# A hybrid encoder block on one core: four PSUM banks each for gates and projections, two lasting value tiles, and values projected last

## The chip, the cores and the metric

The kernel runs on one core of a Trainium2 chip. The metric is the device time of one execution in microseconds (us), from the first to the last instruction and the little around them. The kernel before takes 2870.84 us as the median of 3 runs (2866.83 to 2875.58 us).

The engines of the core are written as in the profile: PE multiplies matrices and adds up in PSUM, PEld loads its weights, DVE, ACT and POOL compute on tiles, SP issues most of the DMA transfers and POOL issues some. PSUM is used here as eight banks of 128 x 512 f32.

## The reference

One layer of an encoder block: 2048 tokens, 1024 channels. The part that the change touches is the input projection and what reads it:

```
xn   = rmsnorm(h, norm_mix_g)
proj = xn @ w_in                                   # 1024 -> 2560 columns
q, k, v, u, y = split(proj, [512, 1024, 1536, 2048])
q, k = rope(q), rope(k)                            # 8 heads x 64
attn = dilated_mixture_attention(q, k, v)          # windows 128/1, 512/4, 2048/16
uc   = centred_depthwise_conv(u, conv_w, conv_b)   # width 4
rec  = bidirectional_rglru(uc, gates ...) * gelu(y)
h    = h + concat([attn, rec]) @ w_out
h    = h + memory_cross_attention(...)             # 256 memory tokens
h    = h + squared_relu_mlp(...)                   # 4096 hidden
```

The two gates of `bidirectional_rglru` are block-diagonal products of `uc` with small weights, for two directions; after them come exponentials and two scans over the sequence.

## The kernel before, in words

**Arithmetic.** Every product of two f32 matrices is made of three matmuls on a high and a low part of each operand (`mm3`, lines 118 to 121: high by high, high by low, low by high). So one output bank of 128 x 512 over 1024 channels takes 8 x 3 = 24 matmuls.

**Stage one, the input projection (about the first 700 us).** The 2048 tokens are held as transposed activations `xh`, `xl` in two blocks of 1024 tokens, block 0 and block 1. Each block has two halves of 512 tokens. The 2560 columns are cut into ten units of 256 columns: two U units and two Y units for the recurrence, and two units each of values (v0, v1), keys (k0, k1) and queries (q0, q1). Each of the last six serves four heads. A unit loads its weights, splits them into `wh` (ACT, L225) and `wl` (POOL or DVE, L226), and then projects:

- `out_unit` (L390) writes one bank of 128 columns x 512 tokens in 24 matmuls. A U or Y unit takes four of them, each read by one DVE instruction (L409) and stored.
- `qk_unit` takes two outputs, `pa` and `pb`, for each half, and calls `rope` (L371 to L388). DVE reads the two banks four times (L376 to L379), adds up (L380, L381); then, for each of two results, ACT makes the high part `rh` (L385), DVE the low part `rl` (L386), and SP stores both (L387, L388) to `q_d` or `k_d` in DRAM. `rh` and `rl` have two buffers each.
- `v_unit` (L431 to L461) goes in four steps of 256 tokens. A step fills one bank in two parts (48 matmuls on 256 columns), DVE scales it into `v` (L451), POOL sets two columns of ones in a tile `vb` (L454), ACT writes the high halves into `vb` (L456), DVE the low ones (L457), and SP stores `vb` to `v_d` (L460). `vb` has one buffer: the memset of a step waits until the stores of the step before it have read the tile.

**The order of the units.** `block` (L575) runs a list of units over one block of tokens. The main sequence (L607 to L637) is: block 0 with U and Y; block 1 with U; the memory's keys and values; block 1 with Y, then the list `QKV` (L573); block 0, loaded a second time, with `QKV` without its last unit; the rest of the recurrence; the loads of head 0; block 0 with the last unit of `QKV`; and then the attention. So the last unit in the list is also the last work on PE before the attention.

**The recurrence beside it.** `lru` (L463 to L547) is a generator: each step of a Y, V, K or Q unit draws 1.3 of its steps. One of its steps is `gates` (L497): two groups of three matmuls, each into a bank of the tag "a", read by ACT (L513 into `tr`, L516 into `ti`), then exponentials on ACT and two DVE products (L520, L521). Other steps are the convolution (L489, L491), the scans (L531, L536) and the final product with the Y branch (L544), stored to `rec_d`.

**PSUM banks.** `psum_phase` opens a set of banks by tag; a tag's tiles rotate over its banks, and a new tile waits until the old tile's readers are done. In stage one the tags are `m0`, `m1`, `b`, `a`, two banks each. A projection asks for "mmb" and gets `m0`, `m1`, `b` in turn, so projections rotate over six banks; the gates have the two of "a". The memory's keys and values use "mm" (`m0`, `m1`) and "b". The profile writes `m` for both `m0` and `m1`.

**What sets the order.** No table of instructions is written out. A tile scheduler orders each engine's instructions from the program's order, the dependencies and the tiles that are free. Each engine then runs its own instructions strictly in that order.

**The start of the attention.** `load_head` (L168) has POOL issue the loads of `qb`, `kh`, `kl` (L175, L178) and SP those of the values (L184 to L193). The attention opens its own banks with `psum_phase("psum2", m0=2, r=1, a=3, b=2)`, in the space that stage one's banks leave. A step is: scores on PE (L750, L751: `a<-kh,qb`), mask and row maximum on DVE (L754), exponentials on ACT (L757). Beside it runs the output projection of the recurrence: a load `rt<-rec_d` (SP, L666), its high part (ACT, L669) and low part (DVE, L670).

Of the kernel before, what the change touches and what calls it, by code (L numbers as in the profile page):

```python
# [10 lines left out]
F32, F32R, F16, BF, I32 = DT.float32, DT.float32r, DT.float16, DT.bfloat16, DT.int32  # L11
# [13 lines left out]
VW = 130  # L25
# [14 lines left out]
def hybrid_block(ctx: ExitStack, tc: tile.TileContext, prm, x, xT, mem, memT, pos, masks, w_in, gate_w,  # L40
# [34 lines left out]

    turn = {"mm": 0, "mmb": 0}

# [9 lines left out]
    def ps(tag):  # L87
        if tag in turn:
            turn[tag] += 1
            tag = ("m0", "m1", "b")[turn[tag] % (2 if tag == "mm" else 3)]  # L90
        return banks["pool"].tile([P, 512], F32, tag=tag, name=tag, bufs=banks[tag])

    def small(name, shape, d=F32):
        return cst.tile(shape, d, name=name)
# [6 lines left out]
    cb, gb, lm, ifq = (col(n) for n in ("conv_b", "gate_b", "lam", "invf"))  # L101
    nhalf = small("nhalf", [P, 4])
    pool.memset(nhalf, -0.5)
    ones = small("ones", [P, 1])
    pool.memset(ones, 1.0)
    all1 = small("all1", [P, P])
    pool.memset(all1, 1.0)
    dsc = small("dsc", [P, 4])
    hpi = small("hpi", [P, 1])
    pool.memset(hpi, TWO_PI / 4)  # L110
# [92 lines left out]

    psum_phase("psum1", m0=2, m1=2, a=2, b=2)
    sh = ExitStack()
    with ExitStack() as s12:
# [56 lines left out]
        def memory_kv(p1):  # L263
# [12 lines left out]
            for c in range(8):  # L276
                if c % 2 == 0 and c > 0:
                    W = unit_w((w_ck if c < 4 else w_cv)[(c % 4) // 2])
                o = ps("mm")
                for k in range(8):  # L280
# [9 lines left out]
                if c < 4:  # L290
                    act.activation(eh, e, AF.Copy)
                    dve.tensor_tensor(el, e, f32(eh), op=ALU.subtract)
                    dma(km_d[0, :, c, :], f32(eh))
                    dma(km_d[1, :, c, :], f32(el))
                else:
                    t = ps("b")
                    for j in range(2):
                        pe.transpose(t[:, 128 * j:128 * j + 128], e[:, 128 * j:128 * j + 128], idt)
                    act.activation(eh, t[:, :256], AF.Copy)
                    dve.tensor_tensor(el, t[:, :256], f32(eh), op=ALU.subtract)  # L300
                    for z, tt in ((0, eh), (1, el)):
                        dma(vm_d[z, :, :, 128 * (c - 4):128 * (c - 4) + 128],
                            f32(tt).rearrange("p (j d) -> p j d", j=2))
# [86 lines left out]
        def out_unit(W, X, c, th):  # L390
            o = ps("mmb")
            for k in range(8):
                mm3(o, *W(k, slice(128 * c, 128 * c + 128)), X[0][th][k], X[1][th][k], k == 0, k == 7)
            return o
# [37 lines left out]
        def v_unit(W, X, B, n2, step, sums):  # L432

            for th in range(2):
                for m2 in range(2):
                    o = ps("mmb")
                    v = p2.tile([P, 512], F32, tag="r0", name="v")
                    for z in range(2):
# [6 lines left out]
                        if sums:  # L445
# [6 lines left out]
                                                 op0=ALU.mult, op1=ALU.mult)  # L452
                    vb = p2.tile([P, 8, VW], F16, tag="vb", name="vb", bufs=1)
                    pool.memset(vb[:, :, 64:66], 1.0)  # L454
                    v3 = v.rearrange("p (h d) -> p h d", h=8)
# [116 lines left out]
        U, Y = [(0, "u", 0), (1, "u", 1)], [(2, "y", 0), (3, "y", 1)]  # L572
        QKV = [(4, "v", 0), (6, "k", 0), (8, "q", 0), (5, "v", 1), (7, "k", 1), (9, "q", 1)]  # L573

        def block(B, X, tabs, units, side, first=None, sums=None):  # L575
# [8 lines left out]
            for n, (wi, kind, n2) in enumerate(units):  # L584
# [15 lines left out]
                if kind == ("y" if B else "v") and n2 == 0:  # L600
                    fill_tables(B, rbn, cosT, sinT)

        none = iter(())
        last = {}
# [32 lines left out]
    with ExitStack() as s3:  # L637
        mk = s3.enter_context(sb("mk"))
        psum_phase("psum2", m0=2, r=1, a=3, b=2)
        pw = s3.enter_context(sb("pw"))  # L640
# [925 lines left out]
```

## Time and profile before

| What | Value |
|---|---|
| Median of 3 runs | 2870.84 us (2866.83 to 2875.58) |
| Profiled execution | 2870.64 us, of which the span from first to last instruction is 2868.9 us |
| Busy PE in the span | 2585.6 us (90%), 14104 recorded matmuls |
| Busy DVE, ACT, POOL | 2027.9 us (71%), 1285.1 us (45%), 1256.8 us (44%) |
| Mean granted PE clock | 0.952 |
| Stage one after its start, 244 to 663 us | 419 us, PE busy 334.4 us |
| Between stage one and the attention, 663 to 704 us | 41 us, PE busy 3.3 us |

All times in the profile are in us from the first instruction of one profiled execution, unless marked ns. A row of a timeline gives the start, the duration, the engine, the line, the operation with output<-inputs, and in brackets how long the engine had stood idle before it and what ended that. A row of the groups gives how often it ran, its busy time in all, the mean ns of one, and then the idle time of the engine just before such instructions with the releasers that ended most of it. The releaser is inferred: it is the wait that ended last by the profile. Row counts can be a few per cent short, since some matmul records are missing.

### The profile page before, as it was taken

Reading aid. Unit: us, or ns where it says so; the run is one execution under the profiler, and the core shown is the slowest. Engines: PE = TensorE matmul, PEld = TensorE weight load, DVE = VectorE, ACT = ScalarE, POOL = GpSimd, SP = SyncE. Lnnn points to the kernel's source line nnn. Section 1 sums busy time; section 2 is a strip of 40 time slices with the busy share of each in tenths; the row PEclk is TensorE's granted clock in tenths of the full one; section 3 lists DMA queues with packets and bytes.
Section 4 is the critical chain, followed back from the end, with each engine's and each line's share of the span. In section 5 each row is a group of like instructions: output and inputs, shape, how many; then the busy total and the mean of one; then the engine's idle time right before and its main releaser. Section 6 shows DMA issues by size and latency. Waiting matters only on the chain. (4 is left out here: it accounts for less than half of the span.)

```text
span 2868.9 us, 40008 instructions
## 1 busy us (share of the span) xinstructions
PE 2585.6 (90%) x14104; PEld 2186.2 (76%) x14104; DVE 2027.9 (71%) x3376; ACT 1285.1 (45%) x2366; POOL 1256.8 (44%) x884
## 2 busy tenths in 40 slices
PE   8899785884889998999997999899998999999997
PEld 6778675774889998787875788778886777777876
DVE  7547676764778878546578544665548999999997
ACT  6438545452556666335433333433333333333342
POOL 2222121211544442451145555646656766666662
PEclk9999897987889999899998999999999999999999
DMA  6433344336677784653243333343335222212213
GB/s 214 144 125 98 116 113 141 101 106 186 180 184 210 201 206 124 202 170 102 97 159 121 108 113 107 113 144 109 109 114 205 71 84 81 81 67 89 77 49 118
DMA packets 258045, 368.43 MB, mean 128 GB/s; under 512 B 85683, under 2 KB 132019, under 8 KB 254773
## 3 DMA queue, kind: packets, MB, share of 16 engines
q1 hardware_dynamic: 253556, 338.62, 37.4%
q0 software_dynamic: 4288, 27.27, 3.8%
q8 instruction: 111, 1.82, 0.3%
q14 instruction: 90, 0.73, 0.1%
HBM read 251.19 MB, written 114.63 MB: 128 GB/s over the span
## 5 line engine op out<-in xcount | busy, mean ns | idle before, releaser
L1299 ACT ACTIVATE c<-raw 128x512 fp32r<-128x512 f32 x162 | 101.8, 632 | 274.0 <-PE m L120 137.4
L1149 ACT ACTIVATE wh<-wr 128x512 fp32r<-128x512 f32 x128 | 80.9, 632 | 288.9 <-PE m L120 145.9
L1150 POOL TENSOR_TENSOR wl<-wr,wh 128x512 fp32r<-128x512 f32 x96 | 144.7, 1508 | 146.3 <-ACT wh L1149 146.3
L757 ACT ACTIVATE sm<-sm,obp 128x256 f32<-128x256 f32 (+1 forms) x384 | 161.4, 467 | 46.2 <-DVE obp L754 40.0
L1150 DVE TENSOR_TENSOR wl<-ws,wh 128x512 fp32r<-128x512 f32 x96 | 82.2, 856 | 126.5 <-ACT wh L1149 117.6
L754 DVE CUSTOM_DVE_ANT_0 sm<-a,msk 128x256 f32<-128x256 f32 (+1 forms) x384 | 131.0, 371 | 31.3 <-PE a L751 27.5
L226 POOL TENSOR_TENSOR wl<-wraw,wh 128x512 fp32r<-128x512 f32 x48 | 70.3, 1467 | 166.5 <-ACT wh L225 157.6
L1171 DVE TENSOR_TENSOR c<-m,c 128x512 f32<-128x512 f32 x64 | 44.2, 690 | 139.9 <-PE m L121 137.9
L769 ACT ACTIVATE ph<-b 128x512 f16<-128x512 f32 (+1 forms) x192 | 100.4, 523 | 95.2 <-PE b L766 90.3
L119 PE MATMUL m<-xh,wh 128*128 128x512 f32 x328 | 131.3, 400 | 7.4 <-ACT xh L320 7.4
L770 DVE SCALAR_TENSOR_TENSOR pl<-b,ph 128x512 f16<-128x512 f32 (+1 forms) x192 | 114.6, 598 | 28.4 <-ACT ph L769 24.5
L120 PE MATMUL m<-xl,wh 128*128 128x512 f32 x328 | 130.1, 397 | 0.7 <-DVE xl L321 0.7
L121 PE MATMUL m<-xh,wl 128*128 128x512 f32 x328 | 130.5, 398 | 0.0
L1300 POOL TENSOR_TENSOR wh<-raw,c 128x512 fp32r<-128x512 f32 x58 | 94.7, 1648 | 76.6 <-ACT c L1299 71.6
L696 POOL TENSOR_SCALAR kc<-kh 128x1024 fp32r<-128x1024 f32 x32 | 68.5, 2141 | 127.7 <-PE a L750 115.6
L766 PE MATMUL b<-prt,sm 128*128 128x128 f32 x640 | 107.8, 283 | 17.3 <-DVE pl L770 9.3
L750 PE MATMUL a<-kc,qb 128*128 128x256 f32 x256 | 108.5, 425 | 5.9 <-DVE obp L754 5.9
L1172 DVE SCALAR_TENSOR_TENSOR c<-c 128x512 f32<-128x512 f32 x96 | 112.4, 1171 | 1.0
L1149 ACT ACTIVATE wh<-ws 128x512 fp32r<-128x512 f32 x96 | 60.3, 628 | 109.0 <-PE m L120 108.0
L121 PE MATMUL m<-t3h,wl 128*128 128x512 f32 x276 | 107.7, 390 | 1.1 <-POOL wl L1150 1.1
L1300 POOL TENSOR_TENSOR wl<-raw,c 128x512 fp32r<-128x512 f32 x58 | 93.3, 1625 | 19.8 <-ACT c L1299 19.8
L751 PE MATMUL a<-kc,qb 128*128 128x256 f32 x256 | 101.6, 397 | 0.0
(571 smaller groups left out, 9731.0 us busy)
## 6 DMA issues: line engine op xcount, KB each, us to landing
wr<-in_w_m SPq DMA_DIRECT2D x64, 512.0 KB
hid_d<-c SPq DMA_DIRECT2D x128, 256.0 KB
wraw<-in_w_in SPq DMA_DIRECT2D x80, 256.0 KB
raw<-in_w_m SPq DMA_DIRECT2D x33, 512.0 KB
rawt<-hid_d SPq DMA_DIRECT2D x26, 512.0 KB
t0h<-hid_d SPq DMA_DIRECT2D x26, 512.0 KB
o_d<-obp SPq DMA_DIRECT2D x16, 528.0 KB
obr<-o_d SPq DMA_DIRECT2D x16, 528.0 KB
```

The source lines that it names most:

```text
L119: pe.matmul(o, ah, bh, start=start, stop=False, **kw)
L120: pe.matmul(o, ah, bl, start=False, stop=False, **kw)
L121: pe.matmul(o, al, bh, start=False, stop=stop, **kw)
L750: pe.matmul(so, q0, kh[:, w0:w0 + 256], start=True, stop=False)
L754: dve.tensor_tensor_reduce(out=sm, in0=sps[:, 256 * z + o0:256 * z + o0 + kw], in1=msk[:, m:m + kw], op0=ALU.add, op1=ALU.min, scale=1.0, ...
L757: exps.append(act.activation(sm, sm, AF.Exp, scale=-1.0, bias=self.obp[:, oc, 65:66]))
L766: pe.transpose(pt[:, c0:c0 + 128], self.sm[:, z, 128 * g:128 * g + 128], idt)
L770: dve.scalar_tensor_tensor(self.pl[:, :w], pt[:, :w], 1024.0, self.ph[:, :w], op0=ALU.mult, op1=ALU.subtract)
L1149: act.activation(h, self.a[n], AF.Copy)
L1150: last[n % 2] = (pool if n % 2 else dve).tensor_tensor(l, self.a[n], f32(h), op=ALU.subtract).ins
L1172: dve.scalar_tensor_tensor(z, z if n < 6 else o, 0.0, z, op0=ALU.max, op1=ALU.mult)
L1300: self.eng[n].tensor_tensor(l[-1], tk, f32(h[-1]), op=ALU.subtract)
```

## The change

Four things change; the computation and its operands stay the same.

1. **Banks.** Stage one has two tags of four banks: "a" for the gates (four instead of two) and "mp" for all projections (four instead of six). The memory's transposes, "b" before, take "a".
2. **Value tiles.** The one-buffer tile `vb` with a memset in each step becomes two tiles that last through stage one. Their ones are set once, ahead of all units; a step takes the two in turn.
3. **Order of units.** `QKV` was v0, k0, q0, v1, k1, q1 and is v0, k0, q0, k1, q1, v1. Both blocks of tokens use it, so v1 is the last projection of block 1 and the last projection of all.
4. **Constants.** The column of ones is a column of the all-ones matrix, and two small constants share a tile (one memset fewer). The attention's `psum_phase` names its banks in another order, `a`, `b`, `m0`, `r`.

```diff
-    turn = {"mm": 0, "mmb": 0}
+    turn = {"mm": 0}
...
-            tag = ("m0", "m1", "b")[turn[tag] % (2 if tag == "mm" else 3)]
+            tag = ("m0", "m1")[turn[tag] % 2]
...
-    ones = small("ones", [P, 1])
-    pool.memset(ones, 1.0)
     all1 = small("all1", [P, P])
     pool.memset(all1, 1.0)
+    ones = all1[:, 0:1]
...
-    psum_phase("psum1", m0=2, m1=2, a=2, b=2)
+    psum_phase("psum1", a=4, mp=4)
...
         def out_unit(W, X, c, th):
-            o = ps("mmb")
+            o = ps("mp")
...
                 for m2 in range(2):
-                    o = ps("mmb")
+                    o = ps("mp")
...
-                    vb = p2.tile([P, 8, VW], F16, tag="vb", name="vb", bufs=1)
-                    pool.memset(vb[:, :, 64:66], 1.0)
+                    vb = vbs[(2 * th + m2) % len(vbs)]
...
-        QKV = [(4, "v", 0), (6, "k", 0), (8, "q", 0), (5, "v", 1), (7, "k", 1), (9, "q", 1)]
+        QKV = [(4, "v", 0), (6, "k", 0), (8, "q", 0), (7, "k", 1), (9, "q", 1), (5, "v", 1)]
...
+        vbs = [p2.tile([P, 8, VW], F16, name=f"vb{i}") for i in range(2)]
+        for vb in vbs:
+            pool.memset(vb[:, :, 64:66], 1.0)
...
-        psum_phase("psum2", m0=2, r=1, a=3, b=2)
+        psum_phase("psum2", a=3, b=2, m0=2, r=1)
```

The scheduler turns this into other orders in stage one; from the first scores on, every engine has the same order as before. The line numbers of the changed kernel are one or two lower in stage one and one higher in the attention. Three places show it.

PE, gate groups in block 1. The names are the bank of the gates (`a_2744` and so on), a projection's bank (`m1`, `b`), the convolved input (`uh`, `ul`) and the gate weights (`gh`, `gl`). Before, the third and the fourth group of a run stand apart, behind some matmuls of a projection:

```order
L121 MATMUL a_2749<-uh_2378,gl_2537 128x512
L119 MATMUL b_2809<-xh_860,wh_2789 128x512
L120 MATMUL b_2809<-xl_861,wh_2789 128x512
L121 MATMUL b_2809<-xh_860,wl_2790 128x512
L119 MATMUL b_2809<-xh_864,wh_2789 128x512
L120 MATMUL b_2809<-xl_865,wh_2789 128x512
L121 MATMUL b_2809<-xh_864,wl_2790 128x512
L119 MATMUL b_2809<-xh_870,wh_2789 128x512
L119 MATMUL a_2763<-uh_2378,gh_2536 128x512
L120 MATMUL a_2763<-ul_2379,gh_2536 128x512
L121 MATMUL a_2763<-uh_2378,gl_2537 128x512
L120 MATMUL b_2809<-xl_871,wh_2789 128x512
```

In the changed kernel the four groups stand together, in four banks:

```order
L120 MATMUL mp_2686<-xh_958,wl_2555 128x512
L118 MATMUL a_2737<-uh_2375,gh_2529 128x512
L119 MATMUL a_2737<-ul_2376,gh_2529 128x512
L120 MATMUL a_2737<-uh_2375,gl_2530 128x512
L118 MATMUL a_2742<-uh_2375,gh_2529 128x512
L119 MATMUL a_2742<-ul_2376,gh_2529 128x512
L120 MATMUL a_2742<-uh_2375,gl_2530 128x512
L118 MATMUL a_2756<-uh_2375,gh_2529 128x512
L119 MATMUL a_2756<-ul_2376,gh_2529 128x512
L120 MATMUL a_2756<-uh_2375,gl_2530 128x512
L118 MATMUL a_2761<-uh_2375,gh_2529 128x512
```

What moved: the second pair of gate groups comes right behind the first, where before single matmuls of a projection lay between them.

DVE, the last rows of stage one and the first of the attention, before. The names are the two banks of q1's last half (`m_5396`, `b`), the rotary tables, and the products and parts made of them:

```order
L376 TENSOR_TENSOR t_5446<-m_5396,cosT 128x512
L378 TENSOR_TENSOR t_5448<-m_5396,sinT 128x512
L377 TENSOR_TENSOR t_5447<-b,sinT 128x512
L379 TENSOR_TENSOR t_5449<-b,cosT 128x512
L380 TENSOR_TENSOR t_5446<-t_5446,t_5447 128x512
L381 TENSOR_TENSOR t_5448<-t_5448,t_5449 128x512
L386 SCALAR_TENSOR_TENSOR rl<-t_5446,rh 128x512
L386 SCALAR_TENSOR_TENSOR rl<-t_5448,rh 128x512
L670 TENSOR_TENSOR rl_6273<-rt,rh_6272 128x1024
L754 ISA sm,obp<-a,msk 128x256
```

The same place in the changed kernel (`mp` is a projection's bank, `vb0` and `vb1` are the two value tiles):

```order
L385 SCALAR_TENSOR_TENSOR rl_5168<-t2_5153,rh_5167 128x512
L450 SCALAR_TENSOR_TENSOR v_5214<-mp_5213,rsb_149,svr1_154 128x256 x2
L455 TENSOR_TENSOR vb0_155<-v_5214,vb0_155 128x8x64
L450 SCALAR_TENSOR_TENSOR v_5270<-mp_5269,rsb_149,svr1_154 128x256 x2
L455 TENSOR_TENSOR vb1_156<-v_5270,vb1_156 128x8x64
L450 SCALAR_TENSOR_TENSOR v_5326<-mp_5325,rsb_149,svr1_154 128x256 x2
L455 TENSOR_TENSOR vb0_155<-v_5326,vb0_155 128x8x64
L450 SCALAR_TENSOR_TENSOR v_5382<-mp_5381,rsb_149,svr1_154 128x256 x2
L455 TENSOR_TENSOR vb1_156<-v_5382,vb1_156 128x8x64
L671 TENSOR_TENSOR rl3_6242<-rt_6239,rh3_6241 128x1024
L755 ISA sm_5467,obp_5465<-a_5466,msk_5177 128x256
```

What moved: the last row `rl` of the query unit now stands ahead of v1's four steps, and the attention's first rows follow the values instead of the rotary work.

POOL, the end of stage one before (`wl` is the low part of a unit's weights, `ti` the recurrence):

```order
L226 TENSOR_TENSOR wl<-wraw,wh 128x512
L454 MEMSET vb 128x8x2
L226 TENSOR_TENSOR wl<-wraw,wh 128x512
L454 MEMSET vb 128x8x2 x2
L226 TENSOR_TENSOR wl<-wraw,wh 128x512 x2
L539 TENSOR_TENSOR ti<-ti 128x1024 x2
L175 DMA qb<-q_d_64 128x2048
```

The same place in the changed kernel:

```order
L225 TENSOR_TENSOR wl<-wraw,wh 128x512 x4
L487 TENSOR_SCALAR uc<-u,prt 128x512
L225 TENSOR_TENSOR wl<-wraw,wh 128x512 x4
L537 TENSOR_TENSOR ti<-ti 128x1024 x2
L174 DMA qb<-q_d_64 128x2048
```

What moved: no memset of a value tile stands on POOL any more between the low parts of the weights.

More of the change, by code (lines that the diff above doesn't have):

```diff
@@ L101, in hybrid_block @@
     cb, gb, lm, ifq = (col(n) for n in ("conv_b", "gate_b", "lam", "invf"))
-    nhalf = small("nhalf", [P, 4])
+    misc = small("misc", [P, 8])
+    nhalf, hpi = misc[:, 0:4], misc[:, 4:5]
     pool.memset(nhalf, -0.5)
-    ones = small("ones", [P, 1])
-    pool.memset(ones, 1.0)
     all1 = small("all1", [P, P])
     pool.memset(all1, 1.0)
+    ones = all1[:, 0:1]
     dsc = small("dsc", [P, 4])
-    hpi = small("hpi", [P, 1])
     pool.memset(hpi, TWO_PI / 4)
@@ L278, in memory_kv @@
                     W = unit_w((w_ck if c < 4 else w_cv)[(c % 4) // 2])
-                o = ps("mm")
+                o = ps("mp")
                 for k in range(8):
@@ L295, in memory_kv @@
                 else:
-                    t = ps("b")
+                    t = ps("a")
                     for j in range(2):
@@ L435, in v_unit @@
                 for m2 in range(2):
-                    o = ps("mmb")
+                    o = ps("mp")
                     v = p2.tile([P, 512], F32, tag="r0", name="v")
```

## The prediction

> **What bounds the kernel now.** The page says first that PE is the engine to follow: it is busy for 90% of the span, DVE for 71%.
>
> ```profile
> span 2868.9 us, 40008 instructions
> PE 2585.6 (90%) x14104; PEld 2186.2 (76%) x14104; DVE 2027.9 (71%) x3376; ACT 1285.1 (45%) x2366; POOL 1256.8 (44%) x884
> ```
>
> So a stage can lose only the time in which its PE stands, or runs at a lower clock. The table by stretches shows where that is. Its columns are the length, the busy times of PE, PEld, DVE, ACT and POOL, the granted clock, the DMA share and GB/s.
>
> ```profile
> 244.00:479.00 235.00, 175.72 (x894) 148.00 (x893) 159.80 (x212) 129.06 (x192) 39.84 (x46) 0.88 0.40 120
> 479.00:663.00 184.00, 158.72 (x825) 136.24 (x825) 129.55 (x164) 91.83 (x129) 43.51 (x36) 0.91 0.42 116
> 663.00:704.00 41.00, 3.27 (x13) 2.71 (x13) 13.16 (x23) 5.22 (x7) 4.10 (x6) 0.59 0.60 171
> 704.00:740.00 36.00, 36.00 (x377) 35.50 (x377) 26.63 (x112) 30.72 (x78) 13.46 (x9) 0.94 0.63 175
> ```
>
> Between the last projection and the attention PE works 3.27 of 41 us; from 704 us on it is full. In the two stretches before it stands for some 60 and 25 us. I read the PE groups of 290 to 705 us next: busy time, mean ns, idle before and its releasers.
>
> ```profile
> L119 PE MATMUL m<-xh,wh 128*128 128x512 f32 x149 | 58.8, 395 | 0.0
> L119 PE MATMUL m<-wh,xh 128*128 128x256 f32 x144 | 44.6, 315 | 31.0 <-ACT wh L225 20.8 <-DVE v L451 10.1
> L119 PE MATMUL a<-uh,gh 128*128 128x512 f32 x48 | 23.0, 480 | 48.2 <-ACT tr L513 36.8 <-ACT ti L516 11.4
> L121 PE MATMUL a<-uh,gl 128*128 128x512 f32 x48 | 21.3, 443 | 0.0
> L120 PE MATMUL a<-ul,gh 128*128 128x512 f32 x48 | 21.2, 441 | 0.0
> L119 PE MATMUL b<-wh,xh 128*128 128x256 f32 x48 | 14.4, 300 | 2.2 <-DVE v L451 2.2
> L750 PE MATMUL a<-kh,qb 128*128 128x256 f32 x8 | 3.8, 477 | 38.1 <-DVE t L378 28.4 <-DVE obp L754 9.7
> ```
>
> PE's idle time has four names: 38.1 us ahead of the first scores, 48.2 us for gate banks whose old contents ACT has not read, 20.8 us for weights, 12.3 us (10.1 + 2.2) behind the values.
>
> **Term 1, the end of the stage: -30 us.** The timeline shows what PE waits for there.
>
> ```profile
> 662.26 0.39 PE L121 MATMUL b<-xh,wl 128*128 128x512 f32 x1
> ...
> 667.96 0.68 DVE L381 TENSOR_TENSOR t<-t,t 128x512 f32<-128x512 f32 x1
> 681.48 0.63 ACT L385 ACTIVATE rh<-t 128x512 fp32r<-128x512 f32 x1 [19.60 <-DMA k_d<-rh]
> 683.95 0.69 DVE L386 SCALAR_TENSOR_TENSOR rl<-t,rh 128x512 fp32r<-128x512 f32 x1 [15.31 <-DMA k_d<-rl]
> 690.29 0.68 DVE L378 TENSOR_TENSOR t<-m,sinT 128x512 f32<-128x512 f32 x1
> 690.41 0.90 SPq L666 DMA_DIRECT2D rt<-rec_d  x1
> 691.03 0.58 PE L750 MATMUL a<-kh,qb 128*128 128x256 f32 x1 [28.38 <-DVE t L378]
> 700.94 1.06 ACT L669 ACTIVATE rh<-rt 128x1024 fp32r<-128x1024 f32 x1 [3.30 <-DMA rt<-rec_d]
> 702.03 1.23 DVE L670 TENSOR_TENSOR rl<-rt,rh 128x1024 fp32r<-128x1024 f32 x1 [1.77 <-ACT rh L669]
> 703.99 0.58 PE L750 MATMUL a<-kh,qb 128*128 128x256 f32 x1 [9.70 <-DVE obp L754]
> ```
>
> The last pair's rotary work is held by `rh` and `rl`, whose two buffers each are still being stored (19.60 and 15.31 us). Until DVE has read the bank (690.29) the first score has no bank. Eight pairs of score matmuls later PE waits again: DVE's mask (L754) stands behind `rl<-rt`, and that behind a load issued at 690.41 that ended ACT's wait at 700.94, 10.5 us later, amid the stores.
>
> With v1 last, q1's rotary work and its stores lie beside v1: 192 matmuls on 256 columns, four steps of 5.8 us (48 x 120 ns; in term 4's rows the first of 24 such matmuls starts at 569.85, the last at 572.61, so 23 intervals take 2.76 us), 23 us in all. The gate banks, which `a` of the attention takes, are free by then, since the recurrence is drained. PE goes straight from values to scores. What remains is the second wait: `rt` stands on SP behind the third value step's stores, so it is issued about 4 us before PE ends (the 5.8 us of the fourth step less some 2 for the third's scaling, copy and difference, an estimate from 0.6 to 0.7 us for each such instruction above); 10.5 us later, 6.5 after that end, come 1.06 of ACT and 1.23 of DVE, 8.8 in all, against 3.3 us of scores (the 3.27 of the table). That leaves 5.5; I take 8, since q1's stores may still delay the load. Bounds: nothing remains (-38), or 10 remains as now (-28).
>
> **Term 2, gates in four banks: -24 us, and -4 by the clock.** With four banks a third and a fourth group need not wait for the `tanh` of the first two. What ACT is late for is often not the gates:
>
> ```profile
> 437.80 0.72 ACT L320 ACTIVATE xh<-xr,prt 128x512 fp32r<-128x512 f32 x1 [14.78 <-DMA xr<-in_xT]
> 438.43 0.67 ACT L513 ACTIVATE tr<-a,gbh 128x512 f32<-128x512 f32 x1
> 439.15 0.80 PE L119 MATMUL a<-uh,gh 128*128 128x512 f32 x1 [11.82 <-ACT tr L513]
> ```
>
> ACT stood 14.78 us behind a load of x, with the gates queued after it, and PE 11.82 us behind ACT. Two more banks let PE pass one such hold-up. But ACT's and DVE's chain keeps its order and length, and the next gates come soon. Bounds: 0 and -48.2. I take half, because where PE gets ahead of DVE it meets term 4. The gate matmuls also run slow after such gaps: 480, 441 and 443 ns against 395 for a projection of the same shape, (85 + 46 + 48) x 48 = 8.6 us; half of it, bounds 0 and -8.6.
>
> **Term 3, value tiles: -6 us.** The memsets of `vb` mark the cycle of a step before.
>
> ```profile
> 607.54 0.12 POOL L454 MEMSET vb<- 128x16 f16 x1 [32.15 <-DMA v_d<-vb]
> 614.90 0.11 POOL L454 MEMSET vb<- 128x16 f16 x1 [5.89 <-DMA v_d<-vb]
> 623.36 0.11 POOL L454 MEMSET vb<- 128x16 f16 x1 [8.36 <-DMA v_d<-vb]
> ```
>
> A store must land before the next step: 7.4 and 8.5 us a step, where PE needs 5.8. Two tiles give that cycle 11.6 us, so PE sets the pace. The 14 memsets saved cost 0.11 us each on POOL, but POOL also waited in them (32.15 us above) with the low parts of weights behind; that is cover, since PE's waits for weights are for ACT's `wh`. PE's 12.3 us are the upper bound; `v` itself still has one buffer, so half. Below: 0.
>
> **Term 4, projections in four banks instead of six: +12 us.** A pair's banks are needed again after one more pair, not two. A pair lasts 48 x 227.5 ns = 10.9 us (the rows at 567.79 and 568.24, two matmuls apart, lie 0.45 apart), and two gate groups behind it take 1.4 (568.24 to 569.85, less one matmul). So a bank must be read within 12.3 us of its pair's end.
>
> ```profile
> 531.96 0.40 PE L119 MATMUL b<-xh,wh 128*128 128x512 f32 x1
> 552.07 0.68 DVE L378 TENSOR_TENSOR t<-m,sinT 128x512 f32<-128x512 f32 x1
> 555.96 0.39 PE L121 MATMUL m<-xh,wl 128*128 128x512 f32 x1
> ...
> 567.79 0.39 PE L119 MATMUL b<-xh,wh 128*128 128x512 f32 x1
> 568.24 0.39 PE L121 MATMUL b<-xh,wl 128*128 128x512 f32 x1
> 569.85 0.28 PE L119 MATMUL m<-wh,xh 128*128 128x256 f32 x1
> ...
> 572.61 0.28 PE L121 MATMUL m<-wh,xl 128*128 128x256 f32 x1
> ...
> 570.94 0.68 DVE L378 TENSOR_TENSOR t<-b,sinT 128x512 f32<-128x512 f32 x1
> 580.60 0.68 DVE L378 TENSOR_TENSOR t<-m,sinT 128x512 f32<-128x512 f32 x1
> ```
>
> In block 0 the rotary tables are made while the first key pairs are projected: their first bank is read at 552.07 to 552.75, though PE began the fifth output, which would need it, at 531.96. With four banks that pair ends at 552.75 + 10.9 = 563.7 instead of 556.35: +7.3. The next pair's bank is read by 571.62 (570.94 + 0.68), 15.3 us after 556.35, against PE's 569.85: +1.8. The pair after it, done at 568.6, is read by 581.3, 12.7 us later: about in time. Three more for other places. Bounds: 0, and +48 if each of the 16 pairs (four units, two blocks, two halves) were as late as the 15.3 us one (3.0 each). I stay near the lower end, since only one of the three rows is clearly late for reasons that stay.
>
> The Trainium skill says in "Perfetto Trace Analysis", section "Matmuls", that independent matmul groups should rotate through different PSUM banks, so that reading one overlaps the next group's matmuls. By it, taking banks from the projections, which are most of this stage, would cost more than my 12 us, and giving them to the gates would gain; it sets no number of banks.
>
> **Nothing for the rest.** The list of PE's waits gives the total, the number and the longest.
>
> ```profile
> PE m L119 <- ACT wh L225: 20.8, 2, 13.1
> ```
>
> The two weight waits (20.8 us) stay: v1's and the others' weights still wait for loads and for ACT, though at another place; bounds 0 to -21 and +13 if the longer of them (13.1) came twice. The constants run before the stage fills. The attention's order is unchanged.
>
> **The sum.** 2870.6 - 30 - 24 - 4 - 6 + 12 = 2818.6, so 2819 us. The profiled execution took 2870.64, the median of the runs is 2870.84, so nothing is to be shifted.
>
> **The rivals.**
>
> *A, only the end of the stage gains (24 in 100).* ACT's and DVE's chains through the gates are unchanged in length, and DVE is busy 129.55 of 184 us. What PE doesn't wait for in a gate bank, it then waits for in `v`, rotary banks or weights. For it: the hold-up at 437.80 has nothing to do with banks. Against: that hold-up is 11.82 of 48.2 us. 2870.6 - 30 - 6 + 12 = 2847.
>
> *B, all waits go and four banks suffice (12 in 100).* 2870.6 - 30 - 48.2 - 8.6 - 12.3 = 2771. For it: PE has the work to fill the gaps. Against: the reads at 552.07 and 570.94 above.
>
> *C, slower: PE waits for late rotary work in four banks (8 in 100).* If every pair is read 15.3 us after its end, 16 x 3.0 = 48, and with nothing won at gates and values: 2870.6 - 30 + 48 = 2889. It decides from 30/16 = 1.9 us a pair, a mean lag of 14.2. For it: the 15.3, with `rh` and `rl` held by stores. Against: the 12.7 right behind it.
>
> ```profile
> 635.36 0.78 POOL L175 DMA_DIRECT2D qb<-q_d  x1
> ```
>
> *D, the end's wait only moves (8 in 100).* The first scores need head 0's keys and queries, and those follow the stores. In the trace POOL issues the loads ahead of the last unit's stores, at 635.36, but if they or `rt` come behind q1's stores, the wait grows from 8 to some 35 us: 2870.6 - 3 = 2868.
>
> **How the numbers follow.** My forecast has 48 in 100, and its own range is 2800 to 2840, from the half values of terms 2 and 4 going up or down by 20. For 8 in 10 the range reaches to A, above 2847, and towards B: 2785 to 2860. One cannot tell less than about 0.3% (8.6 us) from no change here: faster means under 2862, slower over 2879. Faster: 48 + 24 + 12 = 84; within: 8 (D); slower: 8 (C).
>
> **What would show it.** In the profile after: (1) the stretch from the last projection matmul, now a value matmul, to the full attention has under 12 us of idle PE instead of 38.1, and the first wait for scores is for L755 behind `rl<-rt`, not for rotary work; (2) the idle time ahead of the first gate matmul of a group falls from 48.2 to about 24, at means nearer 400 ns; (3) no value step waits for `v_d` stores on POOL, and `v` costs PE some 6 us; (4) new PE waits appear behind rotary reads (L375 to L378), the largest of some 7 us in block 0 behind the tables. I am wrong if waits of (4) add up to over 30 us, or if the end of the stage keeps over 20 us of idle PE.

## The result, and the profile after

The changed kernel takes 2889.11 us (median of 4 runs, 2885.19 to 2893.82) against 2872.2 us of the kernel before (4 runs, 2866.83 to 2875.58). The ratio is 1.0061, with a 95% interval of 1.0038 to 1.0084: **slower by 0.6%**, where 2819 us was forecast. The profiled execution took 2885.19 us. The ratios of the experiments further down are to the kernel before as it ran beside them (medians of 2870.07 to 2870.94 us); two disturbed executions, one of `b_banks` at 3726.1 us and one of the kernel before at 8038.03 us, are left out of them. A profile is of one execution, which need not be near the median: it took 2901.44 us for `b_const`, 2881.59 for `b_order` and 2845.3 for `a_all`. The page of the changed kernel:

```profile
span 2883.4 us, 39981 instructions
PE 2611.4 (91%) x14104; PEld 2191.7 (76%) x14104; DVE 2016.5 (70%) x3376; ACT 1289.1 (45%) x2366; POOL 1261.5 (44%) x869
```

PE has the same 14104 matmuls and is busy for 25.8 us longer. The table by stretches, at the same times as before (length; busy PE, PEld, DVE, ACT, POOL; clock, DMA share, GB/s):

```profile
244.00:479.00 235.00, 178.44 (x910) 153.56 (x908) 166.74 (x222) 139.30 (x206) 46.18 (x40) 0.88 0.41 121
479.00:663.00 184.00, 137.53 (x659) 116.50 (x659) 120.81 (x157) 80.84 (x113) 31.86 (x23) 0.86 0.41 116
663.00:704.00 41.00, 29.33 (x202) 27.87 (x203) 14.63 (x40) 10.22 (x20) 11.22 (x9) 0.82 0.76 182
704.00:740.00 36.00, 34.83 (x370) 33.95 (x367) 28.62 (x102) 28.64 (x73) 18.12 (x11) 1.00 0.70 171
```

The empty 41 us at the end of the stage are full now, but the stretch before them lost 21 us of PE work. PE's groups of 290 to 705 us say where:

```profile
L118 PE MATMUL mp<-xh,wh 128*128 128x512 f32 x234 | 93.4, 399 | 4.3 <-DVE t L377 4.3
L118 PE MATMUL mp<-wh,xh 128*128 128x256 f32 x192 | 62.6, 333 | 88.1 <-DVE v L450 42.4 <-ACT wh L224 35.5 <-DVE t L377 7.7
L118 PE MATMUL a<-uh,gh 128*128 128x512 f32 x48 | 20.5, 427 | 13.7 <-ACT tr L511 10.6 <-ACT ti L514 3.2
L751 PE MATMUL a<-kh,qb 128*128 128x256 f32 x16 | 5.4, 354 | 6.4 <-DVE obp L755 6.3
```

The wait ahead of the scores went from 38.1 to 6.4 us and that for the gates from 48.2 to 13.7. Against that, the waits ahead of value matmuls rose from 33.2 (31.0 + 2.2) to 88.1; the row names 85.6 of these, and the other 2.5 are one wait for a rotary read (`t`, L378). The stage gained only a little: the first attention row on DVE that both kernels have, `rl<-rt,rh`, started at 702.03 before and here starts at 695.50.

```profile
695.50 1.23 DVE L671 TENSOR_TENSOR rl<-rt,rh 128x1024 fp32r<-128x1024 f32 x1 [3.34 <-ACT rh L670]
...
1606.52 0.68 DVE L1173 SCALAR_TENSOR_TENSOR c<-m,c 128x512 f32<-128x512 f32 x1
...
2875.21 1.05 DVE L1418 SCALAR_TENSOR_TENSOR t5l<-t5l,prt,rb 128x256 f32<-128x256 f32 x1 [2.08 <-ACT rb L163]
```

The same two later rows of the kernel before:

```profile
1613.82 0.68 DVE L1172 SCALAR_TENSOR_TENSOR c<-m,c 128x512 f32<-128x512 f32 x1
...
2860.81 1.05 DVE L1417 SCALAR_TENSOR_TENSOR t5l<-t5l,prt,rb 128x256 f32<-128x256 f32 x1 [1.79 <-ACT rb L164]
```

So the changed kernel is 6.5 us ahead after stage one, 7.3 ahead at 1610 us, and 14.4 behind at the end. It loses 21.7 us between 1610 and 2870 us, in the MLP, where no instruction and no order differs. There are two questions: what happened to the MLP, and why stage one gave 6 us instead of 52.

### The profile page after: what moved, and what is told of

Read it like the earlier page. It is cut to its first block, busy times and chain, and to the rows that moved or that the text cites. A ratio compares the mean times of both kernels' runs of the same rounds, so it can differ in the third digit from the quotient of the medians.

```text
span 2883.4 us, 39981 instructions
## 1 busy us (share of the span) xinstructions
PE 2611.4 (91%) x14104; PEld 2191.7 (76%) x14104; DVE 2016.5 (70%) x3376; ACT 1289.1 (45%) x2366; POOL 1261.5 (44%) x869
## 5 line engine op out<-in xcount | busy, mean ns | idle before, releaser
L118 PE MATMUL mp<-xh,wh 128*128 128x512 f32 x512 | 204.0, 399 | 11.9 <-ACT xh L319 7.6
L119 PE MATMUL mp<-xl,wh 128*128 128x512 f32 x512 | 203.4, 397 | 0.3 <-DVE xl L320 0.3
L120 PE MATMUL mp<-xh,wl 128*128 128x512 f32 x512 | 203.4, 398 | 0.0
L758 ACT ACTIVATE sm<-sm,obp 128x256 f32<-128x256 f32 (+1 forms) x384 | 161.9, 468 | 48.7 <-DVE obp L755 42.4
L118 PE MATMUL mp<-wh,xh 128*128 128x256 f32 x256 | 81.1, 322 | 89.2 <-DVE v L450 43.4
L755 DVE CUSTOM_DVE_ANT_0 sm<-a,msk 128x256 f32<-128x256 f32 (+1 forms) x384 | 131.3, 373 | 32.1 <-PE a L752 28.2
L770 ACT ACTIVATE ph<-b 128x512 f16<-128x512 f32 (+1 forms) x192 | 100.5, 523 | 90.7 <-PE b L767 89.6
L771 DVE SCALAR_TENSOR_TENSOR pl<-b,ph 128x512 f16<-128x512 f32 (+1 forms) x192 | 114.9, 599 | 27.4 <-ACT ph L770 23.4
L118 PEld LDWEIGHTS mp<-wh,xh 128*128 128x128 f32 x256 | 56.4, 223 | 94.5 <-DVE v L450 47.1
L118 PEld LDWEIGHTS mp<-xh,wh 128*128 128x128 f32 x512 | 98.1, 192 | 34.0 <-ACT xh L319 7.6
L119 PEld LDWEIGHTS mp<-xl,wh 128*128 128x128 f32 x512 | 98.5, 192 | 22.1 <-DVE xl L320 1.2
L120 PEld LDWEIGHTS mp<-xh,wl 128*128 128x128 f32 x512 | 98.4, 192 | 21.3 <-issue 0.7
```

The source lines that it names most:

```text
L118: pe.matmul(o, ah, bh, start=start, stop=False, **kw)
L119: pe.matmul(o, ah, bl, start=False, stop=False, **kw)
L120: pe.matmul(o, al, bh, start=False, stop=stop, **kw)
L755: dve.tensor_tensor_reduce(out=sm, in0=sps[:, 256 * z + o0:256 * z + o0 + kw], in1=msk[:, m:m + kw], op0=ALU.add, op1=ALU.min, scale=1.0, ...
L758: exps.append(act.activation(sm, sm, AF.Exp, scale=-1.0, bias=self.obp[:, oc, 65:66]))
L770: act.activation(self.ph[:, :w], pt[:, :w], AF.Copy, scale=1024.0)
```

## Experiments on the MLP: addresses in SBUF

Inside the MLP there are stretches in which PE never stands. Here are 200 us of one, before:

```profile
1900.00:2100.00 200.00, 200.00 (x884) 165.52 (x883) 102.63 (x118) 64.89 (x114) 121.24 (x79) 1.00 0.33 111
```

and in the changed kernel:

```profile
1900.00:2100.00 200.00, 200.00 (x859) 161.15 (x858) 95.06 (x113) 65.08 (x113) 116.29 (x75) 1.00 0.31 108
```

PE is busy throughout and the granted clock is 1.00 in both, but 859 matmuls are done instead of 884. From the timeline, a 128x512 matmul starts every 0.227 us before and every 0.233 us after; in stage one it is 0.227 us in both. What differs is where the tiles lie in SBUF, the memory that holds them; the program takes tiles from its left and from its right end. The packed constants, which make room for the second value tile, take two small tiles less, so in the built program every tile on the left side lies 64 bytes lower. In a row `out<-x,w` the first input is the moving operand, which streams through PE, and the second the weights, which are loaded into it. In the MLP the moving operands (`t0h` to `t6l`) and some weights (`c`) are on the left, the other weights (`wh`, `wl`, `ws`) on the right. Modulo 128 bytes the moving operands were at 32 and are at 96; `wh`, `wl` and `ws` are at 32 in both. In stage one, moving operands and weights both lie on the left and moved together.

Four kernels test this. The instructions of each, and their order, are those of the kernel that it is made from, but for the constants that `b_const` packs.

**a_left64**: the changed kernel, with 64 unused bytes on the left from the attention on.

```diff
+    ctx.enter_context(sb("pad")).tile([P, 16], F32, name="pad")
     with ExitStack() as s3:
```

> The changed kernel with one unused tile of 64 bytes a partition opened between the projection stage and the attention. Every instruction, its engine and its order are those of the changed kernel; only the addresses in SBUF of the tiles on the left side, from the attention on, move up by 64 bytes, back to those of the kernel before. Address theory (in the MLP the moving operands lie 64 bytes off, modulo 128, from the weights, which makes a 128x512 matmul start every 0.233 us instead of 0.227): the spacing in the MLP goes back to 0.227 us and some 20 us come back, 2869 us, a little faster than before. Rival (the slow MLP comes from the clock of that run, or from what stage one leaves in the queues): nothing changes, 2889 us and 0.233 us.

Measured: 2865.8 us, ratio to before 0.9986 (0.9972 to 1.0). The MLP is back at 884 matmuls:

```profile
1900.00:2100.00 200.00, 200.00 (x884) 165.55 (x883) 101.23 (x116) 65.76 (x115) 123.64 (x80) 1.00 0.32 110
```

**a_right64**: the changed kernel, with 64 unused bytes on the right instead, so that `wh`, `wl` and `ws` move to 96 as well.

```diff
         kp = sk.enter_context(sb("kp", side="right"))
+        kp.tile([P, 16], F32, name="pad")
```

> The changed kernel with an unused tile of 64 bytes at the start of the right side's pool for the cross attention and the MLP, so that the weights there move by 64 bytes and have the same place modulo 128 as the moving operands (96 and 96). If what matters is that moving operand and weights lie alike modulo 128: 2869 us and a spacing of 0.227 us. If what matters is that the moving operands lie at 96 modulo 128: 2889 us and 0.233 us. If it is not the addresses at all: 2889 us.

Measured: 2863.22 us, 0.9976 (0.9963 to 0.9989). With both at 96 the matmuls are as quick as with both at 32:

```profile
1900.00:2100.00 200.00, 200.00 (x884) 165.62 (x883) 97.70 (x114) 67.80 (x119) 120.41 (x78) 1.00 0.32 112
```

**b_const**: the kernel before, with only the constants packed as in the change.

> The kernel before with only its constants packed as in the change (the column of ones taken from the all-ones matrix, two small tiles made one). It saves two small tiles, so all left-side tiles lie 64 bytes lower. Address theory: 20 us slower than before, 2892 us, with a spacing of 0.233 us in the MLP, and stage one as before. Rival (the change in the MLP comes from banks, values or order): 2872 us.

Measured: 2891.56 us, 1.0083 (1.006 to 1.0105). The constants alone make the kernel before as slow as the changed one:

```profile
1900.00:2100.00 200.00, 200.00 (x859) 161.15 (x858) 97.90 (x114) 64.24 (x111) 117.52 (x76) 1.00 0.31 108
```

**b_left32**: the kernel before, with 32 unused bytes on the left (as in a_left64, with `[P, 8]`): moving operands at 64, `wh`, `wl`, `ws` at 32.

> The kernel before with an unused tile of 32 bytes between the projection stage and the attention: left-side tiles lie at 64 modulo 128, the weights of the MLP at 32. If any difference modulo 64 or 128 costs: about 2892 us, spacing near 0.233 us. If only an offset of 64 counts: 2872 us and 0.227 us.

Measured: 2896.56 us, 1.0097 (1.0081 to 1.0114).

```profile
1900.00:2100.00 200.00, 200.00 (x858) 160.81 (x857) 94.98 (x112) 65.29 (x113) 118.37 (x77) 1.00 0.32 108
```

So it is neither the place 96 nor an offset of exactly 64. In these six kernels the MLP is quick where moving operands and weights have the same address modulo 128, and 3% slower where they have not: alike at (32, 32) in two kernels and (96, 96) in one, unlike at (96, 32) in two and (64, 32) in one. Inside one kernel it shows too, though less sharply. Take the pairs of 128x512 matmuls of 2190 to 2840 us that start less than 0.25 us apart, so that no wait lies between. In `b_left32`, a matmul whose own weights and next weights lie like its moving operand starts the next one after 0.228 us in the mean (647 of them); where the own, the next or both lie otherwise, after 0.232 to 0.234 us (1886). In the changed kernel the first kind takes 0.229 us (651); where only the next weights lie otherwise it is 0.230 (717), and where the own do, 0.233 to 0.234 (1168). In `before` all kinds take 0.227. So there the own weights count for most, and the alike ones are a little slow too. The granted clock is 1.00 in all six rows; the PSUM banks and what stage one leaves behind are excluded by `b_const`, which has none of the other edits. What in the chip makes the difference stays open: only the spacing was measured.

The Trainium skill ("SBUF — State Buffer", section "Who interferes with whom") gives PE two read ports, one for the moving operand and one for loading weights, calls them independent, and says that PE never waits on anyone. It names no address; read so that the two never hold each other up, it would give all six kernels one spacing. The runs differ from that, 884 against 859 matmuls in the same 200 us, and the measurement decides.

## Experiments on stage one: each part alone

With the addresses put back (`a_left64`), the rest of the change is worth some 4 us of 2870 (by the interval of `a_left64`, 0 to 8), not 52. Four kernels take the parts apart, all with the MLP's addresses as before.

**b_order**: the kernel before, with only the new order of units.

```diff
-        QKV = [(4, "v", 0), (6, "k", 0), (8, "q", 0), (5, "v", 1), (7, "k", 1), (9, "q", 1)]
+        QKV = [(4, "v", 0), (6, "k", 0), (8, "q", 0), (7, "k", 1), (9, "q", 1), (5, "v", 1)]
```

> The kernel before with only the order of the units changed (v1 behind q1). Its addresses are those of before. Value-step theory: the second half of a value step goes into the same bank as the first and waits until DVE has read that, so PE can be only 24 matmuls (2.9 us) ahead of DVE; with v1 last, DVE stands behind the last Y loads and the rotary work of q1, so the 30 us won at the end come back as waits inside v1 and for v1's weights: 2870 us (2862 to 2878), with over 15 us of PE waits ahead of v1's matmuls behind L451. Rival (the order gives what was forecast, and the four projection banks took it back): 2840 us, with no such wait.

Measured: 2872.58 us, 0.9998 (0.9978 to 1.0017): no change. PE's groups of 290 to 712 us:

```profile
L119 PE MATMUL m<-wh,xh 128*128 128x256 f32 x112 | 35.6, 326 | 18.0 <-DVE v L451 12.6 <-ACT wh L225 5.4
L119 PE MATMUL b<-wh,xh 128*128 128x256 f32 x80 | 27.3, 342 | 45.3 <-DVE v L451 37.1 <-ACT wh L225 8.2
L119 PE MATMUL a<-uh,gh 128*128 128x512 f32 x48 | 22.9, 478 | 35.8 <-ACT tr L513 26.8 <-ACT ti L516 8.9
L750 PE MATMUL a<-kh,qb 128*128 128x256 f32 x16 | 5.1, 339 | 5.5 <-DVE obp L754 5.5
```

The end of the stage is 5.5 us instead of 38.1, as the order was to do. But the waits behind `v` are 49.7 (12.6 + 37.1) instead of 12.3. With six banks for projections they are as long as in the changed kernel, so the four banks didn't make them.

**b_banks**: the kernel before, with only the banks changed (the lines on `turn`, `psum_phase("psum1", ...)` and `ps(...)` of the change).

> The kernel before with only the banks changed (four for the gates, four for projections). Value-step theory: gate waits fall by some 34 us as in the changed kernel, waits for late rotary reads of some 15 us come new, the end of the stage stays: 2851 us. Rival (four banks are too few for projections): no gain or slower, 2870 to 2889 us, with over 30 us of PE waits behind rotary reads. Rival A of the forecast (the chains behind the gates take it back): 2870 us, with the waits under other names.

Measured: 2874.39 us (median of nine), 1.0003 (0.9985 to 1.002): no change. PE's groups of 290 to 710 us:

```profile
L119 PE MATMUL mp<-xh,wh 128*128 128x512 f32 x236 | 94.3, 399 | 10.0 <-DVE t L378 10.0
L119 PE MATMUL mp<-wh,xh 128*128 128x256 f32 x192 | 60.0, 322 | 44.3 <-ACT wh L225 20.7 <-DVE v L451 18.7 <-DVE t L379 2.5
L119 PE MATMUL a<-uh,gh 128*128 128x512 f32 x48 | 22.1, 463 | 34.0 <-ACT tr L513 25.3 <-ACT ti L516 8.6
L750 PE MATMUL a<-kh,qb 128*128 128x256 f32 x9 | 3.8, 422 | 33.8 <-DVE t L379 24.7 <-DVE obp L754 9.1
```

The gates wait 14.2 us less than before (34.0 against 48.2) and the end 4.3 less (33.8 against 38.1). Rotary reads, new, cost 14.9 (10.0 + 2.5, and 2.4 more that the value row does not name) and `v` 6.4 more (18.7 against 12.3). Before, the named waits add up to 119.4 (48.2 + 20.8 + 12.3 + 38.1); here to 122.1 (34.0 + 20.7 + 18.7 + 14.9 + 33.8). The waiting only changed its name.

**b_vbs**: the kernel before, with only the two lasting value tiles, the constants that make room for them, and the 64 unused bytes of `a_left64`.

> The kernel before with only the two lasting value tiles, the packed constants that make room for them, and an unused tile of 64 bytes behind the projection stage that keeps the addresses of the MLP. Value-step theory: PE's 12 us of waits in the value units are for DVE's reads, not for stores, so little changes, 2867 to 2871 us. Forecast: 6 us less, 2864 us.

Measured: 2868.39 us, 0.998 (0.9957 to 1.0003): unclear; by the interval at most 0.4% faster or 0.03% slower. PE's waits behind `v` are still 10.4 us from 290 to 712 us (12.3 before).

**a_oldorder**: the changed kernel, with the old order of units and the 64 unused bytes.

> The changed kernel with the old order of units (v1 in the fourth place, q1 last) and the unused 64 bytes that keep the MLP's addresses. Value-step theory: the gain of the banks without the waits in v1, but with the end of the stage as before: about 2850 us, faster than the changed kernel with the 64 bytes (2866). Rival (the order is what gains, the banks lose): 2866 + 30 = 2896 us.

Measured: 2875.84 us, 1.0013 (0.9986 to 1.0041): no change against before, where 2850 was expected. Banks and value tiles together win nothing either. The value-step theory, which the runs inside v1 bear out below, had put their gain at 20 us here, and that part of it is wrong.

## Experiments inside v1

Why does PE stand in v1? The timeline of the changed kernel, with SP's stores and loads of the Y branch (SPq is SP issuing a transfer), POOL's first load of head 0, DVE, and PE on both sides of its longest wait:

```profile
632.81 4.07 SPq L543 DMA_DIRECT2D rec_d<-gy  x2
...
636.81 0.78 POOL L174 DMA_DIRECT2D qb<-q_d  x1
...
656.08 1.48 SPq L541 DMA_DIRECT2D gy<-gy_d  x2
...
636.08 0.68 DVE L378 TENSOR_TENSOR t<-mp,cosT 128x512 f32<-128x512 f32 x1
659.13 0.69 DVE L542 TENSOR_TENSOR gy<-ti,gy 128x512 f32<-128x512 f32 x1 [22.38 <-DMA gy<-gy_d]
661.01 0.68 DVE L379 TENSOR_TENSOR t<-t,t 128x512 f32<-128x512 f32 x1
663.66 0.48 DVE L450 SCALAR_TENSOR_TENSOR v<-mp,rsb,svr 128x256 f32<-128x256 f32 x1
...
640.63 0.28 PE L120 MATMUL mp<-wh,xl 128*128 128x256 f32 x1
664.19 0.58 PE L118 MATMUL mp<-wh,xh 128*128 128x256 f32 x1 [23.28 <-DVE v L450]
```

DVE waits 22.38 us for the last loads of the Y branch (`gy`), and the rest of q1's rotary work and v1's first scaling stand behind that in DVE's order. From 635.00 to 640.9 PE had done 48 matmuls of v1, the first half of the first step and, in another bank, the first half of the second. Next in its order is the second half of the first step, and PE stood, although half of that bank was still to be filled: the program lets DVE read the first half before PE writes the second, and PE waits for this read. So PE can be two halves ahead of DVE here, not one as the expectation of `b_order` says. The loads were not under way for 22 us: SP issued them only at 656.08. They go into the tiles that the stores `rec_d<-gy` read, and SP waited 19.1 us for these stores to land (632.81 is their issue). That the stores are late because POOL's loads of head 0 (3 MB) start at 636.81 is a theory at this point. The kernel before had the same hold-up (its DVE waited 11.11 us for `gy` at 652), but there PE was at work on q1. Four edits on `a_left64` test the links.

**a_headsp**: head 0's queries and keys are loaded by SP behind the recurrence's last store.

```diff
-                    dma(rec_d[ct, ...], gy)
+                    last["rec"] = dma(rec_d[ct, ...], gy).ins
...
-        dma_r(t.q, q_d[h // 4][h % 4])
+        ld = dma_r if h else lambda o, i: dma(f32(o), i)
+        ld(t.q, q_d[h // 4][h % 4])
...
-        heads = {0: load_head(hd_p, 0)}
+        with tc.issue_after(last["rec"]):
+            heads = {0: load_head(hd_p, 0)}
```

> The changed kernel with the 64 bytes (2866 us), in which the loads of head 0's queries and keys (3 MB) are issued by SP behind the last store of the recurrence, not by POOL as soon as their data stands. Load theory: POOL's 3 MB at 637 to 640 us hold the last two loads of the Y branch for 22 us, DVE stands with them, and v1, whose every half bank waits for DVE, stands with DVE; without that collision DVE's wait falls from 22 to under 6 us, PE's longest wait in v1 from 24 to under 8, and some 15 us are won: 2851 us. Rival (v1 waits for DVE's own work, the loads are not its cause): 2866 us with the wait of 24 us unchanged.

Measured: 2870.58 us, 0.9999 (0.9982 to 1.0016): nothing won. The waits of 636 to 712 us (total, times, longest):

```profile
PE mp L118 <- DVE v L451: 33.1, 2, 20.8
ACT vb L455 <- DMA v_d<-vb: 23.8, 1, 23.8
DVE vb L456 <- ACT vb L455: 21.5, 4, 19.4
DVE gy L543 <- DMA gy<-gy_d: 12.0, 2, 11.8
```

The first link holds by half: without the collision SP waits 8.3 us for the stores instead of 19.1, DVE's wait for the Y loads falls from 22.4 to 11.8 where under 6 was expected, and PE's first wait in v1 from 24.2 to 12.3. But now head 0's loads stand ahead of v1's value stores in SP's order. SP issues the first of these stores at 684.56, behind a load of head 0's values (`v<-v_d`) whose issue alone lasted 16.22 us, and ACT, DVE and PE wait for the value tile: PE's second wait, 20.8 us. The wait only found another place; why that one issue took so long stays open. The Trainium skill says in "DMA: Bandwidth & Descriptors", section "Issuing engines are not separate DMA queues", that transfers run on the same 16 engines and interleave, whichever engine started them. The first wait agrees: SP's stores took 19.1 us with POOL's 3 MB beside them and 8.3 without.

**a_vsplit**: each half of a value step has a bank of its own.

```diff
-                    o = ps("mp")
...
-                        oz = o[:, 256 * z:256 * z + 256]
+                        oz = ps("mp")[:, 0:256]
```

> The changed kernel with the 64 bytes (2866 us), in which each half of a value step has a PSUM bank of its own. Value-step theory: PE can be four halves ahead of DVE (11.6 us) instead of one (2.9 us); the wait of 24 us in v1 falls to about 15 and the other waits behind L450 (22 us in nine) nearly vanish: 2866 - 9 - 12 = 2845 us. Rival (DVE and the stores set the pace of the stage, PE only stands at another place): 2862 to 2866 us, with the time under other names.

Measured: 2849.58 us, 0.9924 (0.9904 to 0.9943). PE's groups of 290 to 712 us:

```profile
L118 PE MATMUL mp<-wh,xh 128*128 128x256 f32 x192 | 57.3, 307 | 50.4 <-ACT wh L224 23.0 <-DVE v L449 16.2 <-DVE t L377 9.1
L751 PE MATMUL a<-kh,qb 128*128 128x256 f32 x16 | 6.1, 393 | 27.7 <-DVE obp L755 20.4 <-DVE v L449 7.3
```

In `a_left64` the first group is 335 ns and 90.7 us, of it 45.6 behind `v` in eight waits. Here one of these is left, 16.2 us. The last link holds: PE is now up to four halves ahead of DVE, and a bank for each half was worth 16 us (2865.8 to 2849.58). The advice of the Trainium skill that the prediction cited ("Perfetto Trace Analysis", section "Matmuls"), independent groups in different banks, agrees with that. But the gain is not the sum of the waits that went. PE's waits of 250 to 712 us add up to 116.1 us in `a_left64` and to 114.1 here: 29.4 less behind `v` and 11.5 less for weights, but 16 more for gates (29.8 against 13.8) and 22 more ahead of the scores (27.7 against 5.8). PE starts the first score behind that last wait 13.5 us earlier (686.38 against 699.91), so some 11 us of it are time in which PE works: the value matmuls run at 307, 301 and 298 ns instead of 335, 322 and 319. Why they run quicker was not tested.

**a_gyhf**: the product with the Y branch is written over the recurrence's own tile and stored from there, so a Y buffer is free as soon as DVE has read it.

```diff
-                    dve.tensor_tensor(gy, hf[:, sl], gy, op=ALU.mult)
-                    dma(rec_d[ct, ...], gy)
+                    dve.tensor_tensor(hf[:, sl], hf[:, sl], gy, op=ALU.mult)
+                    dma(rec_d[ct, ...], hf[:, sl])
```

> The changed kernel with the 64 bytes (2866 us), in which the recurrence's product with the Y branch is written over the recurrence's own tile and stored from there, so that the two buffers of the Y loads are free at once and not when the stores have landed. Load theory: the last Y loads are issued before POOL's 3 MB, DVE's wait of 22 us goes, 2850 us. If the buffers are not what makes them late: 2866 us.

Measured: 2859.92 us, 0.9944 (0.9924 to 0.9965), some 6 us better than `a_left64`. It wasn't for the reason given: SP issues the last Y loads at 636.64 and no longer waits for the stores, but POOL's loads begin at 636.53, and DVE still waits 19.1 us. Of PE's waits, those for weights fell from 34.5 to 25.3 and the one in v1 from 24.2 to 19.6; what shortened them was not tested.

**a_all**: the three edits together.

> The three edits together (head 0's loads from SP, a bank for each value half, the Y product in place) on the changed kernel with the 64 bytes. If all three waits are real and independent: 2866 - 15 - 20 = 2831 us. If DVE's and the stores' chain sets the stage's end whatever PE does: 2850 us or more, with the first full scores not before 685 us.

Measured: **2833.03 us, 0.9863 (0.9834 to 0.9893)**, the quickest kernel of the study: 1.4% under before and 1.9% under the changed kernel. The value group of 290 to 712 us:

```profile
L118 PE MATMUL mp<-wh,xh 128*128 128x256 f32 x192 | 58.5, 313 | 35.3 <-ACT wh L225 14.4 <-DVE t L379 11.8 <-DVE t L378 9.1
L753 PE MATMUL a<-kh,qb 128*128 128x256 f32 x16 | 6.8, 429 | 18.7 <-DMA kh<-k_d 10.4 <-DVE v L450 7.6 <-DVE obp L757 0.7
```

No value matmul waits for `v` any more. What the SP loads add once PE no longer depends on DVE wasn't run apart.

| Kernel | us | ratio to before (95%) |
|---|---|---|
| changed | 2889.11 | 1.0061 (1.0038 to 1.0084) |
| a_left64 | 2865.8 | 0.9986 (0.9972 to 1.0) |
| a_right64 | 2863.22 | 0.9976 (0.9963 to 0.9989) |
| b_const | 2891.56 | 1.0083 (1.006 to 1.0105) |
| b_left32 | 2896.56 | 1.0097 (1.0081 to 1.0114) |
| b_order | 2872.58 | 0.9998 (0.9978 to 1.0017) |
| b_banks | 2874.39 | 1.0003 (0.9985 to 1.002) |
| b_vbs | 2868.39 | 0.998 (0.9957 to 1.0003) |
| a_oldorder | 2875.84 | 1.0013 (0.9986 to 1.0041) |
| a_headsp | 2870.58 | 0.9999 (0.9982 to 1.0016) |
| a_vsplit | 2849.58 | 0.9924 (0.9904 to 0.9943) |
| a_gyhf | 2859.92 | 0.9944 (0.9924 to 0.9965) |
| a_all | 2833.03 | 0.9863 (0.9834 to 0.9893) |

## Why the prediction was wrong

**Term 1, the end of the stage, -30: right in place, wrong in worth.** PE's wait there fell by 31.7 us (38.1 to 6.4), PE does go straight from values to scores, and the remaining wait is the one named, for L755 behind `rl<-rt`. The step that failed is "q1's rotary work and its stores lie beside v1", with v1 at "23 us in all". v1 took 54 us, from 635.00 to the first score at 689.26, and 27.4 of them are two waits for `v` (23.28 and 4.08). The step put q1's rotary work beside v1 as if they were independent. They share DVE's order, and PE can do only the first halves of two value steps before DVE reads. The order of DVE shown with the change has q1's last `rl` ahead of v1's first `v`. What was not asked is what DVE itself would be waiting for at that point: the Y loads, which the trace before showed as a wait of 11.11 us at 652 with nothing behind it that mattered.

**Term 2, gates, -24 and -4: right as a wait, wrong as time.** The gates' wait fell by 34.5 in the changed kernel and by 14.2 with the banks alone, but `b_banks` won nothing. The step that failed is "I take half": a wait that goes at the gates was taken for time won, and the time won is nothing. That is the mechanism of rival A, which had 24 in 100, though its time, 2847, did not come out either. That the chains of ACT and DVE behind the gates set the pace is an inference from the unchanged sum of the waits; no run shortened these chains. The gates do run quicker (427 against 480 ns).

**Term 3, value tiles, -6: wrong sign.** The waits behind `v` went from 12.3 to 42.4. The two tiles aren't to blame (`b_vbs`: 0.998, unclear); with them in the kernel before, the waits behind `v` are still 10.4 of 12.3 us. The waits in the value units were for DVE's reads of a shared bank, as `a_vsplit` shows; the rows on POOL that the prediction took for the cycle of a step did not set PE's pace.

**Term 4, four projection banks, +12: right as a wait, in part by luck.** Rotary reads made PE wait 14.5 us. The two places in block 0 that the rows named, at 551 and 571 us, gave 3.8 and 0.5 instead of 7.3 and 1.8; the other 10.2 (7.7 + 2.5) came in block 1, at 396 and 385 us, where v1 now follows q1; there the prediction had only its "Three more for other places".

**"Nothing for the rest": wrong twice.** The weight waits rose by 14.7 (20.8 to 35.5), a little past the bound of +13 that was given for them. And "the constants run before the stage fills" looked at the constants' instructions, not at their bytes. Moving every left-side tile by 64 bytes cost the MLP some 20 us: 21.7 by the two rows above, 23 between the changed kernel and `a_left64`. No term, rival or bound held it, and without it the time would have been 2866, still 47 us above the forecast and outside its range, near rival D's 2868 by accident.

The sum as measured, in PE's idle time of stage one: -31.7 (end) - 34.5 (gates) + 30.1 (`v`) + 14.7 (weights) + 14.5 (rotary) = -6.9, and the attention began 6.5 us earlier. Beside that the value matmuls ran slower (333 ns against 315 and 300) and the gates quicker.

**C, the slower rival,** came out in time (2889) by luck and wrong in mechanism: rotary reads made PE wait 14.5 us, not 48, and the time it named was lost in the MLP.

## What to carry to other kernels

An idle stretch is not won by moving work into it until one has asked, for the engine that must free that work's output, what it is waiting for at that time; here DVE stood behind a load that SP could not yet issue, and most of the 30 us came back one unit earlier. When PE's waits for one engine go and the sum of all its named waits stays (119.4 and 122.1), look for what sets the pace behind PE. And before a change is blamed on its own place, compare stretches in which PE never stands: a different count of matmuls there is no matter of waits, and an edit that shifts every later tile by some bytes is one to look at.

## What the runs showed of the hardware

- **Addresses of moving operand and weights.** At a granted clock of 1.00 and with PE never standing, a 128x512 matmul started every 0.227 us where moving operands and weights had the same address modulo 128 bytes (three kernels), and every 0.233 us where they differed by 32 or 64 (three kernels): 884 matmuls against 858 or 859 in 200 us, some 20 us in this kernel's MLP.
- **Large loads hold small transfers of another engine.** With head 0's 3 MB under way, issued by POOL from 636.81 on, SP waited 19.1 us for two stores of 256 KB to land, and 8.3 us with the 3 MB issued later (`a_headsp`). Two loads of 256 KB that SP issued beside them at 636.64 made DVE wait 19.1 us (`a_gyhf`), and 10.9 us with the 3 MB issued later (`a_all`).
